# Hybrid decoder layer: two prompt softmax steps inside the query projection, cached-key scores in pairs of sequences

## The chip, the cores and the metric

The kernel runs on one core of a Trainium2 chip. Its engines are PE (TensorE: matrix products and transposes into PSUM), DVE (VectorE), ACT (ScalarE), POOL (GpSimd) and SP (SyncE, which here only issues DMA transfers). Each engine takes its instructions strictly in the order in which they are queued; semaphores hold an instruction until what it needs is there, and everything behind it on that engine waits too. The metric is the device time of one execution in microseconds (us); lower is better.

## The reference

One decoder layer for a prompt (512 rows of 1024) and a sample group (8 sequences of 4 new rows) with the same weights: a mixer, cross-attention into 256 memory tokens, and a gated ConvFFN. The change lies in the cross-attention:

```
def mem_attend(h, mk, mv, w_mq, w_mo):
    q = (h @ w_mq).reshape(B, T, MEM_HEADS, MEM_HEAD_DIM)        # 4 heads x 256
    s = jnp.einsum('bqhd,bkhd->bhqk', q, mk) * (MEM_HEAD_DIM ** -0.5)
    p = jax.nn.softmax(s, axis=-1)
    o = jnp.einsum('bhqk,bkhd->bqhd', p, mv).reshape(B, T, D_MODEL)
    return o @ w_mo
...
x = x + rms_norm(mem_attend(rms_norm(x, g_mem_pre), mk, mv, w_mq, w_mo), g_mem_post)
```

For the prompt, mk and mv come from the prompt's own memory (computed earlier in the kernel). For the samples they are caches, `cache_mem_k` and `cache_mem_v`: 8 sequences x 256 tokens x 4 heads x 256, 1 MB per sequence each for keys and values, read from HBM in this stage.

## The kernel before

The program is written as a straight sequence of calls. A scheduler orders them per engine when the kernel is built: it follows the written order, but lets an instruction pass others when its inputs and a free buffer are there earlier. `tc.issue_after` and `burst` tie an instruction behind another on the same engine. Tiles come from pools with a fixed number of buffers: `mm` (5 PSUM tiles for products), `W` (4 weight slots, reused here for cached keys and values), `st` (6 staging tiles of 512 KB), `S`, `N` and `Z`. A tile can be written again only when all readers of its former contents are done.

The stage of the change, in the written order:

- Query projection. `gemmB` (L485; L472 for the first four blocks) forms the queries transposed, in 8 column blocks m of w_mq, with 3 products for each pair of operands (high and low parts). `ev_q(m)` takes a block out of PSUM: `qh` on ScalarE (L1429), the low part `ql` on Vector (L1430), and the 32 sample rows `qs` on ScalarE (L1432). For the second four blocks `gemmB` is a generator that yields four times per block, so i = 0..15 counts its quarters.
- `mq_spread(h)`, called when head h's two blocks are out, copies that head's sample queries into block-diagonal tiles `qx`: heads 0 and 1 into the first (L1418), heads 2 and 3 into the second, `both` (L1415). It has 16 copies for heads 2 and 3 each, in four groups g of four.
- The prompt pipe, `prompt = pipe(8, ch_soft, ..., ch_turn, ch_out)`. A step i is half of the prompt rows of head i // 2. `next(prompt)` does `ch_out` of step i - 3, `ch_turn` of step i - 2 and `ch_soft` of step i. `ch_soft`: 12 score products `sca` (L1450), the maximum `cnm` on Vector (L1453), exp on ScalarE (L1456), the reciprocal (L1457) and the scaling of the rows `cp` on Vector (L1459). `ch_turn`: four PE transposes `cpt` of the rows (L1468), split into high and low parts `pT` (ScalarE L146, Vector L147). `ch_out`, every second step: 12 products `cpo` with the values (L1480), split into `oT`.
- The samples. `mk_load(b)` requests the keys of sequence b (L1498), 512 KB at a time: b = 0..2 into staging tiles (`wst`), b = 3..6 into weight slots and b = 7 into an `S` tile (`kvt`). `mk_turn(b)` turns them in place on Vector (L1502). `mk_scores` makes 32 products `ssc` for a sequence (L1519; each stands as two records in the trace) and ScalarE copies them to `sc` (L1521). `mk_sum` sums over groups into `pS` (L1535), `mem_softmax` takes the softmax (`spc`, L1550 to L1556, on Vector and ScalarE), turns it on PE (`spt`, L1565) and copies it into `caz` (L1568), `mv_load(b)` requests the values (L1576), and `mv_out` multiplies (`pso`, L1586).
- Then the output projection with w_mo (`gemmA`, L411 to L413).

Before, the keys' scores are made in two lots, sequences 0 to 2 and 3 to 7, after three prompt steps that stand behind the whole projection. Of head 3's sixteen query copies, eight are on GpSimd, four on Vector (g = 2) and four on ScalarE (g = 3).

Of the kernel before, what the change touches and what calls it, by code (L numbers as in the profile page):

```python
# [18 lines left out]
NB = 8  # L19
# [58 lines left out]
def kernel(ctx: ExitStack, tc: tile.TileContext, I, O):  # L78
    nc = tc.nc
# [22 lines left out]
    def S(shape, dt, name):  # L102
        return sp.tile(list(shape), dt, name=name, tag="S")
# [4 lines left out]
    def T2(shape, name, dt=F32):  # L108
        return t2p.tile(list(shape), dt, name=name, tag="T2")
# [7 lines left out]
    def mmp(name="mm"):  # L117
        return psm.tile([P, 512], F32, name=name, tag="mm")
# [4 lines left out]
    def view(t, off, dims, p=None):  # L123
        a = t.ap[0]
        return bass.AP(t.tensor, t.offset + off, [(a[0], a[1] if p is None else p)] + [tuple(d) for d in dims])

    def v2(t, b):
        return t.rearrange("p (a b) -> p a b", b=b)
# [7 lines left out]
    VCP = nc.vector.tensor_copy  # L136
# [72 lines left out]
    def stage():  # L209
        return stg.tile([P, 1024], F32, name="wst", tag="st")  # L210
# [133 lines left out]
    @contextmanager  # L344
    def burst(ins):

        if ins is None:
            yield
        else:
            with tc.issue_after(ins), tc.high_priority():  # L350
                yield
# [23 lines left out]
    def pipe(n, *stages):  # L375

        for t in range(n + len(stages) - 1):
            for s in reversed(range(len(stages))):
                if 0 <= t - s < n:
                    stages[s](t - s)  # L380
            yield
# [80 lines left out]
    def gemmB(xt, evacs, half_first=False):  # L462

        if half_first:
            slots = [W.get() for _ in evacs]
            for i, (c0, c1) in enumerate(HALF):
                for s, ev in zip(slots, evacs):
                    ps = mmp()[:, :c1 - c0]

                    for k0, l, x in ((0, 0, xt.hi), (0, 1, xt.hi), (4, 0, xt.hi), (4, 1, xt.hi), (0, 0, xt.lo), (4, 0, xt.lo)):  # L470
                        for k in range(k0, k0 + 4):
                            done[0] = mm(ps, lhsT=s[:, l, k, :], rhs=x(k, c0, c1), start=(k == 0 and l == 0 and x == xt.hi),  # L472
                                         stop=(k == 7 and x == xt.lo))
                    if i == 1:
                        W.free()
                    ev(i, c0, c1, ps)
                    yield 2.6
            return
        for ev in evacs:
            s = W.get()  # L480
            ps = [mmp()[:, :c1 - c0] for c0, c1 in HALF]
            for k in range(8):
                for j, (l, x) in enumerate(((0, xt.hi), (0, xt.lo), (1, xt.hi))):
                    for i, (c0, c1) in enumerate(HALF):
                        mm(ps[i], lhsT=s[:, l, k, :], rhs=x(k, c0, c1), start=(k == 0 and j == 0), stop=(k == 7 and j == 2))  # L485
                if k % 2 == 1 and k < 7:
                    yield 1.36
            W.free()
            for i, (c0, c1) in enumerate(HALF):
                ev(i, c0, c1, ps[i])  # L490
            yield 1.36
# [38 lines left out]
    for b in range(2):  # L530
        kept.append(norm_turn(xms[b], P, "g_mem_src", memT, b * P))
        if b == 0:

            t = turned[0].ins
            fill = mmp("fill")
            for _ in range(NFILL):
                with burst(t):
                    t = mm(fill, lhsT=warm[:, 0:P], rhs=warm, start=True, stop=True).ins
# [132 lines left out]
    for c0, c1 in HALF:  # L671
# [5 lines left out]
        t = T2([64, n], "gt")  # L677
# [253 lines left out]
    for g in range(2):  # L931
        for h in range(0, H, 2):
            t = stage().rearrange("p (j b e) -> p j b e", j=2, b=4)
# [38 lines left out]
    t = None  # L972
    for h in range(H):
        with burst(t):
            t = mm(pg[NS * h:NS * h + NS, P:2 * P + 1], lhsT=sm_t[:, h, :], rhs=vNs[:, h, :], start=True, stop=True).ins
    for h in range(H):
        with burst(t):
            t = mm(pg[NS * h:NS * h + NS, 4:12], lhsT=qT[:, h, SEQ:], rhs=nT[:, h, :], start=True, stop=True).ins
    for b in range(NB):
        for h in range(H):  # L980
            with burst(t):
                t = mm(pi[NS * h:NS * h + NS, 0:P], lhsT=qzm[:, 256 * h + b * NS:256 * h + (b + 1) * NS],
                       rhs=csts[b // 4, h][:, b % 4, :], start=(b == 0), stop=(b == NB - 1)).ins
# [313 lines left out]
    prompt = pipe(4 * H, da_soft, lambda i: None, da_turn, da_av, da_end)  # L1297
# [110 lines left out]
    def mq_spread(h):  # L1408

        for g in range(4):  # L1410
            copy = VCP if h == 3 and g == 2 else nc.scalar.copy if h == 3 and g == 3 else nc.gpsimd.tensor_copy
            for j in range(4):
                o, q = slice(NS * g, NS * g + NS), v2(qs[NS * j:NS * j + NS, 2 * h:2 * h + 2].rearrange("p c r -> p (c r)"), TS)
                if h // 2:
                    copy(out=both[o, :, j, :, h % 2, g, :], in_=q.rearrange("p (c n) t -> p c n t", c=2))  # L1415
                else:
                    for c in range(2):
                        copy(out=qx[0][c][o, j, :, h % 2, g, :], in_=q[:, NB * c:NB * c + NB])  # L1418

    def ev_q(m):  # L1420
        if m % 2 == 0:
            qh.append(npool.tile([P, 2, 516], F32R, name="qh", tag="N"))
        if m % 4 == 0:
            ql.append(S([P, 4, SEQ], F32R, "ql"))

        def ev(i, c0, c1, ps):
            n = min(c1, SEQ) - c0
            q = qh[m // 2][:, m % 2, c0:c0 + n]
            nc.scalar.mul(out=q, in_=ps[:, :n], mul=1.0 / 16.0)  # L1429
            STT(out=ql[m // 4][:, m % 4, c0:c0 + n], in0=ps[:, :n], scalar=1.0 / 16.0, in1=f32(q), op0=MUL, op1=SUB)  # L1430
            if i == 1:
                nc.scalar.mul(out=qs[:, m, :], in_=ps[:, n:n + NS], mul=1.0 / 16.0)  # L1432
                if m % 2 == 1:
                    mq_spread(m // 2)
        return ev
# [51 lines left out]
    def two(i):  # L1487

        if i < 3:
            return [stage(), stage()]  # L1490
        t = wp.tile([P, 2, DM], F32, name="kvt", tag="W") if i < 7 else S([P, 2, DM], F32, "kvt")
        return [t[:, 0], t[:, 1]]

    def mk_load(b):

        kst[b] = two(b)
        for c in range(2):
            dma(out=kst[b][c], in_=I["cache_mem_k"][0, b, c * P:(c + 1) * P].rearrange("t h d -> t (h d)"))  # L1498

    def mk_turn(b):  # L1500
        for t in kst[b]:
            nc.vector.transpose(out=t, in_=t)  # L1502

    def mk_scores(bs):

        t = None
        for b in bs:
            ps = mmp("ssc")[:, :256]
            for e in range(2):
                o = ps[:, e * P:e * P + P].rearrange("p (h c t) -> p h c t", h=2, c=2)  # L1510
                for c in range(2) if b < 3 else (None,):
                    for j in range(8):
                        g = NS * (j % 4)
                        if c is None:
                            w, k = o[g:g + NS], view(kst[b][0], 512 * e + NS * j, [(256, 2), (DM, 2), (1, NS)])
                        else:
                            w, k = o[g:g + NS, :, c], view(kst[b][c], 512 * e + NS * j, [(256, 2), (1, NS)])
                        with burst(t):
                            t = mm(w, lhsT=qx[e][j // 4][:, j % 4, b].rearrange("p e g t -> p (e g t)"), rhs=k,  # L1519
                                   start=(j < 4), stop=(j >= 4)).ins  # L1520
            nc.scalar.copy(out=sc[:, b], in_=ps)  # L1521
        return t
# [49 lines left out]
    def mv_load(b):  # L1572

        vts[b] = two(b)
        for c in range(2):
            dma(out=vts[b][c], in_=I["cache_mem_v"][0, b, c * P:(c + 1) * P].rearrange("t h d -> t (h d)"))  # L1576
# [12 lines left out]
    prompt = pipe(8, ch_soft, lambda i: None, ch_turn, ch_out)  # L1589
# [4 lines left out]
    for i, _ in enumerate(gemmB(hqT, [ev_q(m) for m in range(4, 8)])):  # L1594
        if i % 4 == 1 and i < 12:
            mk_turn(i // 4)
        if i % 4 == 3:
            mk_load(3 + i // 4)
    mk_load(7)

    next(prompt)
    next(prompt)
    next(prompt)
    sc = S([P, NB, 256], F32, "sc")
    mk_scores(range(3))
    for b in range(3):
        mv_load(b)
    for b in range(3, 8):
        mk_turn(b)
    t = mk_scores(range(3, 8))  # L1610
    for b in range(3, 8):
        mv_load(b)
    next(prompt)
    mk_sum(t)
    with tc.high_priority():
        az = mem_softmax()
# [203 lines left out]
    for gi, js in enumerate(groups):  # L1820
# [49 lines left out]
        if not last:  # L1870
            behind = []
            for n0 in (0, 512):
# [4 lines left out]
                for i in range(nk):  # L1877
# [3 lines left out]
                    for b in range(4):  # L1881
                        t = one(b, ps[b], i, s)
# [63 lines left out]
        t = chunk(TORD[1], 0)  # L1946

        for n0 in (0, 512):
            with burst(t.ins):
                t = chunk(TORD[0], n0)  # L1950
# [79 lines left out]
```

## Time and profile before

| | before |
|---|---|
| median of 3 runs | 948.5 us (947.84 to 948.78) |
| profiled execution | 948.29 us |
| its span, first to last instruction | 946.5 us |
| PE busy in the span | 915.8 us (97%) |
| Vector busy | 610.4 us (64%) |
| ScalarE busy | 378.1 us (40%) |
| GpSimd busy | 222.5 us (24%) |
| mean granted clock of PE | 0.991 |

The profile is one execution, recorded per engine. A row of the chain reads: start, duration, engine, output tile, line, number of records. A row of the timeline has start, busy time, engine, line, operation, out<-in, the shapes and the count, and in brackets the idle time of the engine before it with what ended it. "issue" means that the engine waited for nothing that the profile shows. PE has its weight loads (PEld) recorded apart from the products. A row of stretches gives for each engine the busy time and the number of records, then the granted PE clock (1 is full speed), the share of time that the DMA engines were busy, and GB/s.

### The profile page before, as it was taken

To read this page: it belongs to the slowest core of one execution; us is meant where nothing else is said; L and a number is where in the kernel's file an instruction comes from. 1 tells how busy PE (TensorE), PEld (TensorE's weight loads), DVE (VectorE), ACT (ScalarE), POOL (GpSimd) and SP (SyncE) were. 2 spreads that over 40 slices of the span, in tenths; PEclk is the share of its full clock that TensorE was granted. 3 is DMA by queue.
4 is the path that set the end of the run, shared out by engine and by line. 5 is a ranking of instruction groups with operands and counts; after the bars stand their busy time and mean duration, and the time that the engine had idled before them with its cause. 6 is when DMAs were issued, how large, how long until landed. Compare 5 with 4: busy or idle time off the path is not lost.

```text
span 946.5 us, 17459 instructions
## 1 busy us (share of the span) xinstructions
PE 915.8 (97%) x6778; PEld 800.7 (85%) x6778; DVE 610.4 (64%) x1134; ACT 378.1 (40%) x724; POOL 222.5 (24%) x474
## 2 busy tenths in 40 slices
PE   8999999999999999995999999999999999999994
PEld 5899787889866778995777899989988998999974
DVE  5845145565886448675554778737758775676767
ACT  5745134344676357513444533332212222222232
POOL 6610000025432217371000444001100110110114
PEclk9999999999999999998999999999999999999998
DMA  9950023343870539865854733062053303413023
GB/s 285 308 186 2 2 88 137 89 134 130 280 253 7 177 99 339 261 227 198 311 178 121 208 130 90 18 171 82 5 155 110 96 24 105 141 48 89 24 93 116
DMA packets 120835, 130.59 MB, mean 138 GB/s; under 512 B 8600, under 2 KB 86265, under 8 KB 120753
## 3 DMA queue, kind: packets, MB, share of 16 engines
q1 hardware_dynamic: 114568, 125.96, 42.5%
q10 hardware_dynamic: 6184, 3.53, 1.2%
q8 instruction: 53, 0.87, 0.4%
q14 instruction: 30, 0.24, 0.1%
HBM read 112.54 MB, written 16.93 MB: 137 GB/s over the span
## 4 chain that ended last, share of the span: by engine, by line
PE 86%; DVE 6%; DMA 3%; ACT 1%; issue 1%; POOL 0%; SPq 0%; DVEq 0%; ACTq 0%; POOLq 0%
PE mm L485 32%; PE mm L412 7%; PE mm L413 7%; PE mm L411 7%; PE mm L472 6%; PE mm L1836 3%; PE mm L1840 3%; PE mm L1839 3%; PE sda L1256 2%; PE mm L390 1%; PE cpo L1480 1%; PE sca L1450 1%; PE ssc L1519 1%; PE oda L1284 1%; DVE wslot L147 1%
## 5 line engine op out<-in xcount | busy, mean ns | idle before, releaser
L485 PE MATMUL mm<-fT,wslot 128*128 128x256 f32 x1872 | 235.9, 288 | 0.0
L485 PEld LDWEIGHTS mm<-fT,wslot 128*128 128x128 f32 x1872 | 234.4, 188 | 1.8 <-issue 0.8
L146 ACT CAST wslot<-wst 128x1024 fp32r<-128x1024 f32 x125 | 130.3, 1049 | 252.6 <-issue 77.4
L147 DVE TENSOR_TENSOR wslot<-wst,wslot 128x1024 fp32r<-128x1024 f32 x125 | 154.3, 1240 | 76.8 <-ACT wslot L146 76.6
L1836 PE MATMUL mm<-wslot,act 128*128 128x512 f32 (+1 forms) x180 | 69.3, 387 | 0.0
L1839 PE MATMUL mm<-wslot,act 128*128 128x512 f32 (+1 forms) x172 | 67.0, 391 | 0.0
L1840 PE MATMUL mm<-wslot,act 128*128 128x512 f32 (+1 forms) x172 | 66.8, 392 | 0.0
L1738 POOL COPY cvo<-u 128x2 f32<-128x2 f32 x43 | 10.5, 243 | 217.0 <-DVE u L1736 217.0
L411 PE MATMUL mm<-wslot,hT 128*128 128x512 f32 x128 | 51.3, 402 | 0.0
L413 PE MATMUL mm<-wslot,hT 128*128 128x512 f32 x128 | 51.0, 399 | 0.0
L485 PE MATMUL mm<-hT,wslot 128*128 128x256 f32 (+1 forms) x384 | 50.9, 289 | 0.0
L412 PE MATMUL mm<-wslot,hT 128*128 128x512 f32 x128 | 50.8, 397 | 0.0
L485 PEld LDWEIGHTS mm<-hT,wslot 128*128 128x128 f32 x384 | 49.2, 188 | 0.5 <-issue 0.2
L1733 DVE TENSOR_TENSOR u<-mm,rsb 128x256 f32<-128x256 f32 x43 | 18.2, 424 | 48.8 <-PE mm L485 48.7
L1836 PEld LDWEIGHTS mm<-wslot,act 128*128 128x128 f32 x180 | 34.3, 191 | 8.0 <-issue 0.4
L1840 PEld LDWEIGHTS mm<-wslot,act 128*128 128x128 f32 x172 | 32.3, 188 | 6.9 <-issue 0.4
L1839 PEld LDWEIGHTS mm<-wslot,act 128*128 128x128 f32 x172 | 32.3, 188 | 6.9
L1750 ACT ACTIVATE c<-c 128x560 f32<-128x560 f32 x21 | 14.1, 672 | 56.8 <-DVE c L1744 56.7
L1744 DVE SCALAR_TENSOR_TENSOR c<-u,cvT,c 128x560 f32<-128x560 f32 x43 | 34.3, 798 | 0.9
L1743 DVE SCALAR_TENSOR_TENSOR c<-u,cvT,c 128x560 f32<-128x560 f32 x43 | 34.1, 794 | 0.2
L1851 DVE TENSOR_TENSOR yp<-mm,yp 128x512 f32<-128x512 f32 (+1 forms) x41 | 27.1, 673 | 5.1 <-PE mm L1840 5.1
L413 PEld LDWEIGHTS mm<-wslot,hT 128*128 128x128 f32 x128 | 24.1, 188 | 5.0
(494 smaller groups left out, 1863.7 us busy)
## 6 DMA issues: line engine op xcount, KB each, us to landing
wst<-in_w_up_dram SPq DMA_DIRECT2D x42, 512.0 KB
wst<-in_w_in_dram SPq DMA_DIRECT2D x28, 512.0 KB
wst<-in_w_down_dram SPq DMA_DIRECT2D x20, 512.0 KB
kvt<-in_cache_mem_k_dram SPq DMA_DIRECT2D x10, 512.0 KB
kvt<-in_cache_mem_v_dram SPq DMA_DIRECT2D x10, 512.0 KB
wst<-in_w_mk_dram SPq DMA_DIRECT2D x8, 512.0 KB
xb<-in_x_prompt_dram SPq DMA_DIRECT2D x8, 512.0 KB
wst<-in_cache_dk_dram SPq DMA_DIRECT2D x16, 256.0 KB
```

What stands on the lines that cost most here:

```text
L146: nc.scalar.copy(out=hi, in_=src)
L147: (eng or nc.vector).tensor_tensor(out=lo, in0=src, in1=f32(hi), op=SUB)
L411: mm(ps[b], lhsT=xt.hi(k, c0, c0 + n), rhs=s[:, 0, kk, :], start=(k == 0), stop=False)
L412: mm(ps[b], lhsT=xt.hi(k, c0, c0 + n), rhs=s[:, 1, kk, :], start=False, stop=False)
L413: return mm(ps[b], lhsT=xt.lo(k, c0, c0 + n), rhs=s[:, 0, kk, :], start=False, stop=(k == nk - 1))
L472: done[0] = mm(ps, lhsT=s[:, l, k, :], rhs=x(k, c0, c1), start=(k == 0 and l == 0 and x == xt.hi), stop=(k == 7 and x == xt.lo))
L485: mm(ps[i], lhsT=s[:, l, k, :], rhs=x(k, c0, c1), start=(k == 0 and j == 0), stop=(k == 7 and j == 2))
L1743: STT(out=c, in0=u[:, 1:EXT - 1], scalar=w[1], in1=c, op0=MUL, op1=ADD)
L1744: STT(out=c, in0=u[:, 0:EXT - 2], scalar=w[0], in1=c, op0=MUL, op1=ADD)
L1836: mm(ps, lhsT=t[:, 0, c0:c0 + P], rhs=s[:, 0, i % 2, cs], start=st, stop=False)
L1839: mm(ps, lhsT=t[:, 0, c0:c0 + P], rhs=s[:, 1, i % 2, cs], start=False, stop=False)
L1840: return mm(ps, lhsT=t[:, 1, c0:c0 + P], rhs=s[:, 0, i % 2, cs], start=False, stop=en)
```

## The change

It does four things. The first two prompt steps move into the second half of the projection: after quarter 9 (middle of block 6) and after quarter 13 (middle of block 7). The scores of the cached keys are made in pairs of sequences, (0, 1), (2, 3), (4, 5), (6, 7), with one prompt step after each of the first three pairs, and the values of a pair are requested right behind its scores. The keys of sequences 3 to 7 are turned between the pairs in the written order. And the four copies of head 3's queries with g = 2 go from Vector to ScalarE.

```diff
     def mq_spread(h):
         for g in range(4):
-            copy = VCP if h == 3 and g == 2 else nc.scalar.copy if h == 3 and g == 3 else nc.gpsimd.tensor_copy
+            copy = nc.scalar.copy if h == 3 and g > 1 else nc.gpsimd.tensor_copy
...
     for i, _ in enumerate(gemmB(hqT, [ev_q(m) for m in range(4, 8)])):
...
         if i % 4 == 3:
             mk_load(3 + i // 4)
+        if i in (9, 13):
+            next(prompt)
+
     mk_load(7)
-
-    next(prompt)
-    next(prompt)
     next(prompt)
     sc = S([P, NB, 256], F32, "sc")
-    mk_scores(range(3))
-    for b in range(3):
+    for b in range(0, NB, 2):
+        t = mk_scores((b, b + 1))
         mv_load(b)
-    for b in range(3, 8):
-        mk_turn(b)
-    t = mk_scores(range(3, 8))
-    for b in range(3, 8):
-        mv_load(b)
-    next(prompt)
+        mv_load(b + 1)
+        if b < 6:
+            if b:
+                mk_turn(b + 2)
+            mk_turn(b + 3)
+            next(prompt)
     mk_sum(t)
```

What the scheduler makes of it is seen in the queues. On PE, the cached keys' scores stood in two runs of 96 and 80 products with three transposes between them (before):

```order
L1519 MATMUL ssc<-wst,qx 32x2x32 x96
L1468 MATMUL cpt<-cpk,cp 128x128 x3
L1519 MATMUL ssc<-kvt,qx 32x128 x80
L1468 MATMUL cpt<-cpk,cp 128x128 x4
```

After the change, PE has at the second pair (sequence 2 from staging tiles, sequence 3 from a slot), with prompt products on both sides:

```order
L1450 MATMUL sca<-mkT,ql 128x256
L1519 MATMUL ssc<-wst,qx 32x2x32 x32
L1519 MATMUL ssc<-kvt,qx 32x128 x16
L1480 MATMUL cpo<-pT,mvN 128x512 x12
L1468 MATMUL cpt<-cpk,cp 128x128 x4
```

No run of scores has more than 64 products now, and each is followed by value products, transposes or prompt scores.

On Vector, at the end of the query projection (before; the first row is the evacuation of block 6's queries, the third that of block 7's):

```order
L1430 SCALAR_TENSOR_TENSOR ql<-mm,qh 128x256 x2
L1502 STREAM_TRANSPOSE kvt<-kvt 128x1024 x3
L1430 SCALAR_TENSOR_TENSOR ql<-mm,qh 128x256 x2
L1453 TENSOR_REDUCE cnm<-sca 128x2
L1502 STREAM_TRANSPOSE kvt<-kvt 128x1024
L1415 COPY qx<-qs 32x2x8x4 x4
L1453 TENSOR_REDUCE cnm<-sca 128x2
L1502 STREAM_TRANSPOSE kvt<-kvt 128x1024
L1457 RECIPROCAL csu<-csu 128x2
```

The same place after the change:

```order
L1430 SCALAR_TENSOR_TENSOR ql<-mm,qh 128x256 x2
L1502 STREAM_TRANSPOSE kvt<-kvt 128x1024 x2
L1453 TENSOR_REDUCE cnm<-sca 128x2
L1502 STREAM_TRANSPOSE kvt<-kvt 128x1024
L1457 RECIPROCAL csu<-csu 128x2
L1502 STREAM_TRANSPOSE kvt<-kvt 128x1024
L1459 TENSOR_SCALAR cp<-cp,csu 128x256 x2
L1430 SCALAR_TENSOR_TENSOR ql<-mm,qh 128x256 x2
L147 TENSOR_TENSOR pT<-cpt,pT 128x256
L1453 TENSOR_REDUCE cnm<-sca 128x2
```

Block 7's evacuation now stands behind the second prompt step's maximum, reciprocal and scaling and behind both transposes of sequence 7's keys; the four query copies are gone from Vector. The transposes of sequence 6's keys follow next, and on SP the request of these keys stands behind six loads of the convolution's state.

On PE, around the turned sample softmax `spt` (before):

```order
L1480 MATMUL cpo<-pT,mvN 128x512 x8
L1565 MATMUL spt<-cpk,spc 32x32 x32
L1480 MATMUL cpo<-pT,mvN 128x512 x4
L1468 MATMUL cpt<-cpk,cp 128x128 x4
L1450 MATMUL sca<-mkT,qh 128x256 x2
```

The same place after the change:

```order
L1480 MATMUL cpo<-pT,mvN 128x512 x12
L1468 MATMUL cpt<-cpk,cp 128x128 x4
L1565 MATMUL spt<-cpk,spc 32x32 x32
L1586 MATMUL pso<-wst,caz 32x256 x24
L1468 MATMUL cpt<-cpk,cp 128x128 x4
```

The value products of the samples (`pso`) follow `spt` directly; before, four prompt products, four transposes and twelve prompt scores lay between. Vector's last softmax step (L1556) now stands behind the output difference of the first of the twelve `cpo` groups, and two scaling pairs where there was one.

## Prediction

> **What bounds the kernel now.** I read the page first: the span and the busy shares.
>
> ```profile
> span 946.5 us, 17459 instructions
> PE 915.8 (97%) x6778; PEld 800.7 (85%) x6778; DVE 610.4 (64%) x1134; ACT 378.1 (40%) x724; POOL 222.5 (24%) x474
> ```
>
> PE is the bound: it is idle for 30.7 us of the span and nothing else is near it. So the change can win only PE's idle or slow time. The waits of PE, longest first, say where most of the idle time is: one wait of the prompt's transposes (cpt) for the scaled softmax rows (cp).
>
> ```profile
> PE cpt L1468 <- DVE cp L1459: 7.5, 1, 7.5
> ```
>
> Third, the chain that ended last, from the end of the query projection on (start, duration, what).
>
> ```profile
> 424.12 3.54 DMA kvt<-in_cache_mem_k_dram
> ...
> 427.79 1.25 DVE kvt L1502
> 429.03 0.64 DVE ql L1430 x2
> 429.67 0.60 DVE cnm L1453
> ...
> 432.20 1.84 DVE qx L1415
> ...
> 437.68 0.45 PE cpt L1468
> 438.13 2.56 PE sca L1450 x12
> 440.69 2.53 PE ssc L1519 x160
> 443.22 1.68 issue
> 444.90 0.65 PE ssc L1519 x32
> 445.55 0.48 PE cpt L1468 x3
> 446.03 2.75 PE ssc L1519 x93
> 448.78 3.06 issue
> 451.83 3.36 PE ssc L1519 x67
> 455.19 0.59 PE cpt L1468 x4
> 455.78 1.43 PE sca L1450 x12
> 457.21 2.39 PE pS L1535 x32
> 459.60 2.99 PE cpo L1480 x12
> ...
> 468.18 0.69 PE spt L1565 x50
> ...
> 471.85 2.73 PE pso L1586 x48
> ```
>
> The reader is to see three losses. PE stands still from 437.68 - 7.5 = 430.1 while Vector turns keys, copies queries (1.84 for one copy) and only then scales the softmax rows. Then the twelve score products take 2.56 us, though the same twelve take 1.43 at 455.78. And the cached keys' scores (ssc) stop twice, 1.68 and 3.06 us, waiting for nothing that the profile shows; the 67 records after the second stop take 3.36 us where 93 took 2.75. The clock column (next to last but two) of the stretches of 5 us explains the slow ones:
>
> ```profile
> 435.00:440.00 5.00, 2.32 (x11) 2.35 (x12) 3.32 (x8) 0.83 (x4) 0.00 (x0) 0.50 0.17 39
> 450.00:455.00 5.00, 3.17 (x67) 2.90 (x67) 0.00 (x0) 0.74 (x2) 0.00 (x0) 0.66 0.88 324
> ```
>
> The granted clock is halved after the first standstill and for part of the time after the last.
>
> **What the change removes.** Two prompt steps stand inside the projection, so their scaled rows are ready when PE first wants to turn them, and scores come in four short runs. Against full-speed rows:
>
> - the standstill: 7.5;
> - its slow clock: 2.56 - 1.43 for the scores, and 0.3 for the lone transpose (0.45, where four take 0.59): 1.4;
> - the two stops: 1.68 + 3.06 = 4.7;
> - slow records after the second: 3.36 - 67 x 2.75/93 = 1.4.
>
> Together 15.0 us. The two steps' own 2 x 1.43 us only change place on PE: projection and both steps still end at 430.1.
>
> **What it adds.** (1) The queries of the last head. The scores need qx complete, and the last head's part hangs on the projection's last evacuation. In the new Vector order this evacuation (ql) stands behind the transposes of sequence 7's keys and a softmax scaling. These rows price the pieces:
>
> ```profile
> 429.71 0.20 ACT L1432 ACTIVATE qs<-mm 128x32 f32<-128x32 f32 x1 [1.86 <-DVE ql L1430]
> 429.99 1.04 ACT L1415 COPY qx<-qs 32x64 f32<-32x64 f32 x4
> 429.96 2.17 POOL L1415 COPY qx<-qs 32x64 f32<-32x64 f32 x8 [5.71 <-ACT qs L1432]
> 432.20 1.80 POOL L1558 MEMSET caz<- 128x2048 f32 x1
> 437.20 1.12 DVE L1459 TENSOR_SCALAR cp<-cp,csu 128x256 f32<-128x256 f32 x4
> ```
>
> Sequence 7's keys landed at 424.12 + 3.54 = 427.66. Their buffer comes free in the middle of the last query block, which now has one prompt step more ahead of it: 427.66 + 1.43 = 429.1. Vector: two transposes, 2 x 1.25, to 431.6; half of the 1.12 scaling, to 432.2; ql, 0.64, to 432.8. ScalarE: qs 0.20, which waits for ql as its row shows, and now eight copies, 2 x 1.04, to 435.1; GpSimd's eight take 2.17, beside them. With some 0.05 us for each of six hand-overs: 435.4. PE comes there at 430.1 + 0.59 + 1.43, does the first sixteen products, which need only heads 0 and 1 (0.5, as 32 of 160 records in 2.53), and stands at 432.6. Wait: 2.8, rounded up to **3.0** because the second half of these keys may land later than the first. Bounds: 1.0, if Vector is free when the projection ends (then only ql, qs and the copies remain, 430.1 to 433.3, and hand-overs); 4.0, if the keys land a microsecond later. That two copies leave Vector is worth nothing beyond this: the row of 1.84 ran beside the 1.80 memset of GpSimd, which the new order puts later.
>
> (2) The clock after that wait. The nearest row is the 3.06 stop, with 1.4 us lost after it. I take **1.3**; bounds 0 and 1.4. [...]
>
> (3) The stops. Between them PE ran 32 + 3 + 93 = 128 product records, each with a weight load: 256. The page's instruction queue and two windows of the DMA view (441 to 443, 448 to 452):
>
> ```profile
> q8 instruction: 53, 0.87, 0.4%
> q8 instruction: 1, 0.02, 4.2%
> q8 instruction: 1, 0.02, 1.4%
> ```
>
> 2 x 6778 PE records over 53 packets are 256 each, and one packet lies in each of the two windows, just before PE goes on. So I read the stops as waits for code: 256 records took 3.7 us from block to block the first time (128 records before 443.22 at 2.53/160 each, plus 1.68) and 0.65 + 0.48 + 2.75 + 3.06 = 6.9 the second time, with the DMA engines full of values. In the new order the densest 128 products after the first loads of values are about 111 score records, four transposes and twelve prompt scores: 111 x 2.75/93 + 0.59 + 1.43 = 5.3 us. Cost: 0 to 1.6; the loads of values run there, so nearer the second row: **1.2**.
>
> (4) The sample softmax. Rows, Vector's first, then ScalarE's:
>
> ```profile
> 459.71 0.42 DVE L1552 TENSOR_REDUCE spc<-pS 128x4 f32<-128x256 f32 x1 [1.60 <-PE pS L1535]
> ...
> 463.25 0.69 DVE L147 TENSOR_TENSOR oT<-cpo,oT 128x512 fp32r<-128x512 f32 x1 [0.31 <-ACT oT L146]
> ...
> 467.05 0.40 DVE L1556 TENSOR_TENSOR spc<-spc 128x256 f32<-128x256 f32 x1
> ...
> 472.49 0.41 DVE L147 TENSOR_TENSOR pT<-cpt,pT 128x256 fp32r<-128x256 f32 x1
> ...
> 471.84 0.37 ACT L146 CAST pT<-cpt 128x256 fp32r<-128x256 f32 x1 [0.92 <-DVE pT L147]
> ...
> 468.97 0.43 ACT L1568 COPY caz<-spt 128x128 f32<-128x128 f32 x2 [0.80 <-PE spt L1565]
> ```
>
> On Vector it took 459.71 to 467.45, 7.7 us, under 468.18 - 459.60 = 8.6 us of prompt work on PE. The new order puts three more things ahead of its last step (L1556): one output difference (0.69), one of P (0.41), one scaling pair (0.56). 7.7 + 1.7 = 9.4. PE's cover has 17 value products for 20 (-0.75) and four transposes more (+0.5): 8.35. PE waits **1.1** for spt (0.8 to 1.4, as Vector's own idle in that stretch shrinks or not). Then pso follows spt at once; before, products and a prompt step lay between. The copies of spt (0.43) now stand on ScalarE behind a cast that waits for Vector's next output and P differences: 0.69 + 0.41 + 0.37 + 0.43 and hand-overs, 2.0, less spt's own 0.8: **1.2** more (0.5, if only the copy shows, to 1.5). Two idle pieces so near each other may halve the clock: **0.4** (0 to 1.4).
>
> (5) At nothing: the values' loads now wait each for its own pair's scores, the last at about 453, and are needed past 468; a load of this size took 3.54. GpSimd's memset of 1.80 comes later but long before 468. The output projection's weights wait for pso to free staging buffers:
>
> ```profile
> 479.59 4.63 DVE L147 TENSOR_TENSOR wslot<-wst,wslot 128x1024 fp32r<-128x1024 f32 x4 [0.38 <-ACT wslot L146]
> ```
>
> The first is ready at 479.6 + 1.2, 6.2 us after pso's first run ends (471.85 + 2.73). In the new order 0.59 + 80 x 2.73/48 + 2.99 = 8.1 us of PE work lie there: covered with 1.9 to spare. If that cover went, the projection would start late by the difference.
>
> Sum: 15.0 - (3.0 + 1.3 + 1.2 + 1.1 + 1.2 + 0.4) = 15.0 - 8.2 = 6.8 us. PE stays the bound afterwards, so it reaches the end. The profiled execution took 948.29 (span 946.5 and 1.8 around it): 941.5. It is 0.2 below the median of the three runs, so **941.7** against 948.5. All low ends together give 938, all high ends 946.
>
> **Rivals.** Faster: Vector is free earlier and code is hidden. Then (1) falls to 1.0, and (2) and (3) vanish: 941.7 - 4.5 = 937.2. For it: Vector was idle in front of transposes before, waiting for keys; against: it now has two softmax steps to do in the same stretch.
>
> The stops remain. If they belong to the score products and not to code, shorter runs do not cure them: 1.68 + 3.06 + 1.4 come back in place of (3): 941.7 + 6.1 - 1.2 = 946.6. For it: nothing names the releaser. Against: the 256 records. [...]
>
> Slower: sequence 6's keys. They are requested behind six small convolution loads, and Vector's queue holds their transposes ahead of P's second difference, which a PSUM tile of the next scores waits for (needed at 435.4 + 0.5 + 1.0 + 1.3 + 0.6, about 439). Two transposes and the difference, 2.9, stand between: each microsecond of landing past 436 costs one. Slower than 950.4 needs 8.7 lost, a landing at about 445: against it, 3.54 from request to landing, and even twice that from 430.1 is 437.2. It would give 951.
>
> **How the numbers follow.** Forecast 0.62 (939 to 946); faster rival 0.15; stops remain 0.16; keys late 0.07. The range goes from the fast rival to past the third: 937.0 to 947.5. What a measurement tells from no change is about 0.2%, 1.9 us: faster is below 946.6. The forecast, the fast rival and a third of the stops' case give 0.82; the rest of that case and a little of the last, 0.12; slower 0.06.
>
> **What would show it.** PE's 7.5 wait for cp gone and the two score groups among L485; a PE wait of about 3 us in ssc for qx, released by ScalarE or GpSimd; "issue" in ssc under 2 us in all; waits of about 1 us each ahead of spt and pso; the output projection (L411) starting some 5 us earlier. Wrong would be: a stop of 2 us or more in the new ssc runs without a releaser, a wait in the projection itself for a PSUM tile that Vector has not freed, or gains there that come back as waits in the output projection.

## The result and the profile after

| | before | after |
|---|---|---|
| median | 948.78 us (947.84 to 951.18, 5 executions) | 943.26 us (941.59 to 945.0, 5 executions) |
| ratio to before, 95% interval | | 0.994 (0.992 to 0.9959) |
| profiled execution, its span | 948.29, 946.5 us | 941.59, 939.8 us |
| stage: first product of the second half of the query projection (L485) to the first `rsb` (L1704) | 403.18 to 540.1: 136.9 us | 403.90 to 534.0: 130.1 us |
| the rest, from there to the end of the span | 406.4 us | 405.8 us |

The forecast was 941.7 us, 937.0 to 947.5, faster with 0.82: the measured median is 1.6 us above it. The stage row gives the comparison free of what varies ahead of it (in the profiles shown here, the second half of the projection starts anywhere from 402.95 to 405.02 us in kernels that share the code up to there).

The page after: PE is still the bound, with 1.3 us less busy time and 5.4 us less idle time.

```profile
span 939.8 us, 17453 instructions
PE 914.5 (97%) x6778; PEld 799.9 (85%) x6778; DVE 608.5 (65%) x1130; ACT 378.2 (40%) x728; POOL 221.6 (24%) x474
```

The waits of PE that the stage has now (line, releaser, us in total, times, longest). The wait for `cp` and the "issue" of 4.7 us are gone; these three stand in their place.

```profile
PE ssc L1519 <- POOL qx L1415: 3.7, 1, 3.7
PE pso L1586 <- ACT caz L1568: 1.0, 1, 1.0
PE spt L1565 <- DVE spc L1556: 0.8, 1, 0.8
```

The new largest wait, in the timeline of Vector, ScalarE, GpSimd and PE (start, duration, engine, line, count, and in brackets the engine's idle time before it and what ended it):

```profile
433.07 1.25 DVE L1502 STREAM_TRANSPOSE kvt<-kvt 128x1024 f32<-128x1024 f32 x1 [1.43 <-DMA kvt<-in_cache_mem_k_dram]
434.24 0.57 DVE L1459 TENSOR_SCALAR cp<-cp,csu 128x256 f32<-128x256 f32 x2
434.73 0.74 DVE L1430 SCALAR_TENSOR_TENSOR ql<-mm,qh 128x256 fp32r<-128x256 f32 x2
435.50 0.20 ACT L1432 ACTIVATE qs<-mm 128x32 f32<-128x32 f32 x1 [3.26 <-DVE ql L1430]
435.76 2.16 POOL L1415 COPY qx<-qs 32x64 f32<-32x64 f32 x8 [10.94 <-ACT qs L1432]
432.86 0.65 PE L1519 MATMUL ssc<-wst,qx 128*32 128x64 f32 x32
437.19 3.56 PE L1519 MATMUL ssc<-wst,qx 128*32 128x64 f32 x96 [3.67 <-POOL qx L1415]
```

It is the chain that the prediction set out: transposes of sequence 7's keys, scaling, `ql`, `qs`, copies. Only the keys' second half landed 1.43 us after Vector was ready for it. The 96 records behind the wait take 3.56 us, where 160 took 2.53 before. In part they wait for one copy after another, in part the clock is halved (stretches of 5 us; the granted clock stands before the DMA share and GB/s), from 437.88 to 441.29. The last two rows are PE's alone, for the stretch ahead of the slow one and for the slow one:

```profile
435.00:440.00 5.00, 2.81 (x82) 2.44 (x86) 4.41 (x9) 3.78 (x15) 1.82 (x8) 0.79 0.53 144
440.00:445.00 5.00, 5.00 (x138) 4.50 (x128) 1.83 (x5) 2.15 (x8) 0.00 (x0) 0.87 0.89 291
434.46:437.88 3.42, 0.69 (x6) 1.00 0.67 198
437.88:441.29 3.41, 3.41 (x95) 0.50 0.46 117
```

PE does not wait for all copies: it goes on at 437.19, while GpSimd copies until 435.76 + 2.16 = 437.92.

The two smaller waits, and the output projection's first product, which started at 486.16 before:

```profile
469.10 0.76 PE L1565 MATMUL spt<-cpk,spc 128*32 128x32 f32 x64 [0.84 <-DVE spc L1556]
470.82 2.80 PE L1586 MATMUL pso<-wst,caz 128*32 128x256 f32 x48 [0.96 <-ACT caz L1568]
481.49 0.63 PE L411 MATMUL mm<-wslot,oT 128*128 128x512 f32 x2
```

### The profile page after: what moved, and what is told of

Its sections match the earlier page's. It is cut to its first block, busy times and chain, and to the rows that moved or that the text cites. A ratio compares the mean times of both kernels' runs of the same rounds, so it can differ in the third digit from the quotient of the medians.

```text
span 939.8 us, 17453 instructions
## 1 busy us (share of the span) xinstructions
PE 914.5 (97%) x6778; PEld 799.9 (85%) x6778; DVE 608.5 (65%) x1130; ACT 378.2 (40%) x728; POOL 221.6 (24%) x474
## 5 line engine op out<-in xcount | busy, mean ns | idle before, releaser
L485 PE MATMUL mm<-fT,wslot 128*128 128x256 f32 x1872 | 236.0, 288 | 0.0
L485 PEld LDWEIGHTS mm<-fT,wslot 128*128 128x128 f32 x1872 | 234.4, 188 | 1.8 <-issue 0.8
L1738 POOL COPY cvo<-u 128x2 f32<-128x2 f32 x43 | 10.4, 242 | 217.2 <-DVE u L1736 217.2
L485 PE MATMUL mm<-hT,wslot 128*128 128x256 f32 (+1 forms) x384 | 50.9, 289 | 0.0
L485 PEld LDWEIGHTS mm<-hT,wslot 128*128 128x128 f32 x384 | 49.2, 188 | 0.5 <-issue 0.2
```

## Experiments

Each was timed beside the kernel before on the same chip (whose median there was 948.5 to 950.8 us); the ratio is to those executions. "Stage" is the profiled execution's, as above; the waits are PE's, in us.

| kernel | median us | ratio (95%) | stage | cpt for cp | ssc for qx | issue in ssc | spt + pso |
|---|---|---|---|---|---|---|---|
| before | 948.78 | 1 | 136.9 | 7.5 | 0 | 4.7 | 0 |
| after | 943.26 | 0.994 (0.992 to 0.9959) | 130.1 | 0 | 3.7 | 0 | 1.8 |
| after, measured again | 942.84 | 0.9933 (0.9913 to 0.9954) | 131.3 | 0 | 3.3 | 0 | 1.8 |
| steps only | 944.33 | 0.9935 (0.991 to 0.996) | 131.0 | 0 | 3.5 | 2.1 | 0 |
| pairs only | 944.11 | 0.9943 (0.9924 to 0.9962) | 132.5 | 5.9 | 0 | 0 | 1.8 |
| copies back on Vector | 944.12 | 0.9928 (0.9902 to 0.9955) | 131.7 | 0 | 3.3 | 0 | 1.8 |
| last query first | 940.76 | 0.9882 (0.9851 to 0.9912) | 130.3 | 0 | 1.3 | 0 | 1.8 |
| sample softmax first | 939.69 | 0.9916 (0.9902 to 0.993) | 127.7 | 0 | 3.0 | 0 | 0.4 |
| sample rows first | 939.3 | 0.9895 (0.9872 to 0.9918) | 127.1 | 0 | 0.4 | 0 | 1.8 |
| sample rows and softmax first | 937.49 | 0.989 (0.9874 to 0.9905) | 125.5 | 0 | 0.2 | 0 | 0.4 |

### The steps alone

The kernel before, with only this:

```diff
+        if i in (9, 13):
+            next(prompt)
...
     mk_load(7)
-    next(prompt)
-    next(prompt)
     next(prompt)
```

> The kernel before with only the two prompt steps moved into the query projection (after quarters 9 and 13); scores still in lots of three and five sequences, copies on Vector. Theory (the two edits act apart: the steps remove the standstill, the short runs remove the code stops): the 7.5 us wait of cpt for cp and its slow clock (1.4) go; a wait of about 3.5 us for qx and about 1.5 us of slow clock come; 176 score products now follow each other without anything between, so 'issue' in ssc stays at 4 to 7 us in all. Net gain 3 to 4: 944.5 to 946. Rival (the stops were an after-effect of the standstill, and go with it): no 'issue' over 0.5 us in ssc, and the gain is 9 to 10: 939 to 940.

Measured 944.33 us. The standstill went and the wait for `qx` came, 3.45 us, as expected by the theory; of the stops one remained, 2.15 us, less than the 4 to 7 expected. PE's rows:

```profile
437.41 5.23 PE L1519 MATMUL ssc<-wst,qx 128*32 128x64 f32 x159 [3.45 <-DVE qx L1415]
447.45 2.16 PE L1519 MATMUL ssc<-kvt,qx 128*32 128x128 f32 x67 [2.15 <-issue]
```

The stop stands 67 records before the end of the scores, exactly where the second one stood before. The first had no chance to show: the wait of 3.45 us lies in the 128 records that end where it stood, and most of the rest ran at half clock (5.23 us for 159, where 160 took 2.53 before), so they took 7.7 us, where the 128 up to the second stop before took 6.9 with the stop at their end: time enough for the next code, by the prediction's reading of the stops. So the steps remove part of the stops by themselves (4.7 - 2.15 = 2.6 us, and 3.36 - 2.16 = 1.2 us of the slow records behind the second), and that is why the two halves of the change do not add.

### The pairs alone

The kernel before, with the new loop over pairs of sequences; the first three steps stay behind the projection and the four copies stay on Vector.

```diff
     next(prompt)
     next(prompt)
     next(prompt)
...
-    mk_scores(range(3))
-    for b in range(3):
+    for b in range(0, NB, 2):
+        t = mk_scores((b, b + 1))
         mv_load(b)
-    for b in range(3, 8):
-        mk_turn(b)
-    t = mk_scores(range(3, 8))
-    for b in range(3, 8):
-        mv_load(b)
-    next(prompt)
+        mv_load(b + 1)
...
```

> The kernel before with only the scores in pairs of sequences between prompt steps; the first two prompt steps still behind the projection, copies on Vector. Theory: the wait of cpt for cp stays at 7 to 8 us with its half clock, the wait for qx stays hidden behind it (under 0.5 us), 'issue' in ssc is under 0.5 us in all, and the waits of spt and pso (together about 1.8 us) come: a gain of 6.1 - 1.8 = 4.3, so 944 to 945. Rival (the stops belong to the score products themselves): 'issue' of 3 to 5 us stays in ssc, and the time is 948 to 950.

Measured 944.11 us, as the theory has it: no stop, the two new waits of 0.84 and 0.96 us, and the standstill (5.9, somewhat short of the 7 to 8 expected).

```profile
437.47 0.45 PE L1468 MATMUL cpt<-cpk,cp 128*128 128x128 f32 x1 [5.92 <-DVE cp L1459]
440.41 2.22 PE L1519 MATMUL ssc<-wst,qx 128*32 128x64 f32 x128
471.04 0.76 PE L1565 MATMUL spt<-cpk,spc 128*32 128x32 f32 x64 [0.84 <-DVE spc L1556]
```

By the stage, the steps alone are worth 6.0 us, the pairs alone 4.4, and both 6.8 (5.6 when measured again), not 10.4. With the steps in place the pairs add 0.9 us or nothing: they take away the stop of 2.15 and give back 1.8 at `spt` and `pso`.

### The copies

```diff
-            copy = nc.scalar.copy if h == 3 and g > 1 else nc.gpsimd.tensor_copy
+            copy = VCP if h == 3 and g == 2 else nc.scalar.copy if h == 3 and g == 3 else nc.gpsimd.tensor_copy
```

> The changed kernel with the four query copies of g = 2 back on Vector. Theory: the wait for qx ends with GpSimd's eight copies (2.16 us) whatever ScalarE does, so the wait stays at 3.5 to 4 us and the time at 942 to 944, ratio to the changed kernel 0.998 to 1.002; Vector's four copies (about 1 us) only delay sequence 6's transposes, which cost nothing. Rival (taking the copies off Vector pays by itself): 1 to 2 us slower than the changed kernel, 944.5 to 945.5, with a wait of PE for a tile that Vector frees.

Measured 944.12 us. The wait is 3.3 us, and one of Vector's copies ends it now, not GpSimd's as the theory had it; it is no longer for that. So the move of the copies off Vector is worth nothing that this can tell, as the theory and the prediction had it.

### Whether ql sets qx

```diff
     def mk_turn(b):
-        for t in kst[b]:
-            nc.vector.transpose(out=t, in_=t)
+        with tc.issue_after(qlast[0].ins) if b == 7 else nullcontext():   # the last ql
+            for t in kst[b]:
+                nc.vector.transpose(out=t, in_=t)
```

> The changed kernel with the transposes of sequence 7's keys tied behind the last query evacuation (ql) on Vector. Theory (the wait for qx hangs on ql, which stands behind two transposes of 1.25 us and a wait of 1.4 us for their keys): ql ends about 2.7 to 3.9 us earlier, the wait for qx falls from 3.7 to 0 to 1.2 us, no half-clock window follows (1.5 us), and the time is 4 to 5 us below the changed kernel: 938 to 940. Rival 1 (GpSimd's or ScalarE's copies are the bound): the wait stays over 2.5 us, time within 1 us of the changed kernel. Rival 2 (the delay moves on to the turned keys): the wait for qx falls, but PE waits 2 us or more for kvt of sequences 6 and 7 at the last pair, time 941 to 943.

Measured 940.76 us, a little above the 938 to 940 expected and 3.4 below "copies back" on the same chip. The wait fell to 1.27 us and the records behind it ran at full clock; nothing came back at the last pair. But the profiled execution's stage is only as long as after's (130.3), because it lost 1.7 us at another place, and 1.2 us of waiting for an earlier `ql`:

```profile
436.13 2.34 PE L1520 MATMUL ssc<-wst,qx 128*32 128x64 f32 x96 [1.27 <-POOL qx L1415]
467.16 0.76 PE L1566 MATMUL spt<-cpk,spc 128*32 128x32 f32 x64 [0.84 <-DVE spc L1557]
468.88 4.48 PE L1587 MATMUL pso<-wst,caz 128*32 128x256 f32 x48 [0.96 <-ACT caz L1569]
```

The same 48 records of `pso` took 2.80 us in the kernel after. The waits ahead of them are the same to 0.01 us. The stretches that end with the clock's changes tell the difference (us, PE busy, granted clock, DMA share, GB/s), for this kernel and then for the one after:

```profile
465.66:469.07 3.41, 1.61 (x73) 1.00 1.03 420
469.07:472.48 3.41, 3.41 (x36) 0.50 0.59 187
```

```profile
465.18:468.60 3.42, 3.08 (x16) 1.00 1.03 411
468.60:472.01 3.41, 1.95 (x88) 1.00 0.50 195
```

In this stage the clock changed only at borders a whole number of 3.41 us apart (it was halved from 433.86 to 440.69 and from 450.93 to 454.34 before, from 437.88 to 441.29 after), and these lie elsewhere against the kernel's work from profile to profile. Here both waits fell into one such window, PE was busy for 1.61 us of it, and the next window ran at half clock (0.50). After, a border lay elsewhere, the same waits left 1.95 us busy, and the clock stayed at 1.

### What the stops are

First the values' loads were written behind all scores (in the kernel before):

```diff
-    for b in range(3):
-        mv_load(b)
...
-    for b in range(3, 8):
+    for b in range(8):
         mv_load(b)
```

> The kernel before with all eight sequences' values requested behind the last score product instead of behind each lot. Theory (the two stops are waits for the next block of code, stretched by the values' loads that keep the DMA engines full): with the engines free the 128 records between the two stops take longer (3.9 us) than a quiet fetch (3.7 us from block to block), so the second stop falls from 3.1 us to under 0.6 and the 1.4 us of slow records behind it go; the first stop, which had little traffic, stays between 1 and 2 us. Rival (the stops belong to the score products or to their result tiles): 1.7 and 3.1 us as before, at the same places. In both, the values come some 7 us later, and PE may wait for them in pso, so the time itself (945 to 950) does not decide.

Measured 948.37 us. The edit did not do what it was for. SyncE's queue only waits for free buffers, so the loads still ran beside the scores (DMA share 1.00 below), and the stops were 0.79 and 3.61 us. With a ratio of 0.9997 (0.9985 to 1.0008) the time tells nothing apart either.

```profile
450.00:455.00 5.00, 2.03 (x73) 1.76 (x65) 0.58 (x2) 1.02 (x3) 0.00 (x0) 1.00 1.00 387
455.64 3.47 PE L1519 MATMUL ssc<-kvt,qx 128*32 128x128 f32 x67 [3.61 <-issue]
```

The second try issued them from ScalarE, behind its copy of the last scores:

```diff
+            done[0] = nc.scalar.copy(out=sc[:, b], in_=ps).ins
...
+    with tc.issue_after(done[0]):
+        for b in range(8):
+            mv_load(b)        # nc.scalar.dma_start
```

> The kernel before with all values' loads issued from ScalarE's queue, tied behind its copy of the last sequence's scores, so that none can start before the score products are done. Theory (the stops are waits for the next block of code, stretched by these loads): at both borders the DMA engines are now nearly idle; the first stop, after 160 records, falls from 1.7 to 1 us or less and the second, 67 records before the end, from 3.1 to 1 us or less. Rival (fetching a block takes that long on quiet DMA engines too): stops of 1.5 us or more at the same places. ScalarE issues 16 transfers ahead of its next work and the values come some 8 us later, so the time will be worse (950 to 960) in both and decides nothing.

Now the DMA engines are quiet at both borders (share 0.01 in the stretch), the first stop is 0.91 us and the second is gone: the 160 records run through at the pace of the undisturbed ones before (4.74 us; 160 x 2.75/93 = 4.73). The time, 959.42 us, is worse for the reason given: PE waits 10.6 us for a cast that stands behind ScalarE's sixteen loads.

```profile
446.29 0.65 PE L1519 MATMUL ssc<-wst,qx 128*32 128x64 f32 x32 [0.91 <-issue]
447.36 4.74 PE L1519 MATMUL ssc<-kvt,qx 128*32 128x128 f32 x160
445.00:450.00 5.00, 4.09 (x158) 3.68 (x150) 0.85 (x2) 2.14 (x6) 0.00 (x0) 1.00 0.01 3
```

Third, the place. 64 products ahead of everything shift PE's stream by 128 records against the blocks (their results are not used):

```diff
+    for _ in range(64):
+        mm(wps[:, :8], lhsT=warm[:, 0:P], rhs=warm[:, :8], start=True, stop=True)
```

> The kernel before with 64 tiny extra products (8 columns, result never used) in the warm-up at the very start: 128 more records in PE's stream, half a block of 256. Theory (stops stand at the borders of code blocks): both borders move 64 product records earlier, so the first stop comes after about 96 score records instead of 160, and the second one 131 records before the end of the scores instead of 67; packets of the instruction queue move with them. Rival (the stops belong to the scores' tiles or to their place in the program): both stops stay after 160 records and 67 before the end. Time within 2 us of the kernel before in both.

```profile
449.08 3.05 PE L1521 MATMUL ssc<-wst,qx 128*32 128x64 f32 x192
452.06 0.55 PE L1470 MATMUL cpt<-cpk,cp 128*128 128x128 f32 x3
452.53 1.07 PE L1521 MATMUL ssc<-kvt,qx 128*32 128x128 f32 x29
455.50 5.36 PE L1521 MATMUL ssc<-kvt,qx 128*32 128x128 f32 x128 [1.90 <-issue]
461.69 0.41 PE L1521 MATMUL ssc<-kvt,qx 128*32 128x128 f32 x3 [0.83 <-issue]
```

The stops moved: none after 160 records or 67 before the end. They stand after 192 + 3 + 29 = 224 records and 128 later, which are the expected borders (96, 224, 352). At 96, where the expectation wanted the first stop, there is none: the standstill of 8.1 us lies in the block before that border, and the packet of the next block landed at 437.69, some 13 us before PE came to it. Both points show code and not the scores' tiles. The time, 954.55 us, was expected within 2 us of before and was not: this kernel's projection half starts 7.3 us later (410.50), while its stage (137.6) is before's. What of those 7.3 us the 64 products cost themselves, and what comes from borders that moved ahead of it, no run separates.

The instruction queue shows the link itself. It has one packet for each 128 products with their weight loads (53 packets before, for 6778 products). Eight such stops stand in these profiles: two each in the kernel before, with later values and with shifted code, one each in the steps alone and with the values behind. In all eight PE goes on 1.4 to 1.6 us after the packet of the next block has landed, whether the stop lasted 0.79 or 3.61 us. The second stop before is an example: its packet ran from 449.40 to 450.31, and PE went on at 451.83. What differs is how late the packet starts: 0.6 to 1.1 us behind the border before it with the DMA engines idle or half busy, 1.9 to 5.1 us with them at 0.88 of their time or more.

The same count finds the borders where nothing stopped. These are the 128 products up to the second stop before, and the densest 128 of the kernel after and of the pairs alone (us, PE busy, granted clock, DMA share, GB/s):

```profile
444.90:451.83 6.93, 3.88 (x128) 0.94 0.97 359
450.17:455.49 5.32, 5.32 (x138) 1.00 0.96 357
452.10:457.42 5.32, 5.32 (x137) 1.00 1.04 409
```

The DMA engines were as full in all three (a packet is counted whole where it starts, so a share can pass 1). After, the next packet still came early, from 449.68 to 450.72: the DMA engines had been idle from 448 to 449 (share 0.01), between the loads of two pairs' values. In the pairs alone it landed at 455.79, so with the 1.4 to 1.6 us that follow the code was there at most 0.2 us before PE came to the border.

### The two waits at the sample softmax

The kernel after, with three orders fixed: Vector's L1556 ahead of the `oT` differences, ScalarE's `caz` copies ahead of the next casts, and of the two copies the one that VORD needs first.

```diff
+            with tc.issue_after(smx[0]) if i == 5 else nullcontext():    # L1556
                 put(oT, h // 2, j, j + 1, 0, SEQ, po.unsqueeze(1))
...
+        with tc.issue_after(smx[1]) if i == 6 else nullcontext():        # the caz copies
             for c in range(2):
                 split(...)                                               # cpt to pT
...
-        for c in range(2):
+        for c in (1, 0):
             nc.scalar.copy(out=view(az, c * 1024, ...
```

> The changed kernel with three orders fixed by hand: Vector's last sample softmax step (L1556) ahead of the output differences that stood before it, ScalarE's copies of spt into caz ahead of the casts of the next transposes, and the copy that the first value product needs made first. Theory (the two waits come from what is queued ahead on Vector and ScalarE): the wait of spt falls from 0.8 to under 0.3, that of pso from 1.0 to 0.6 or less, and no half-clock window follows them: 1 us less than the changed kernel's best executions, 1.5 to 2 in the mean, ratio to the kernel before 0.991 to 0.993. Rival (the chain of the softmax itself is that long): both waits stay near 0.8 and 1.0, ratio 0.994.

Measured 939.69 us. `spt` no longer waits and `pso` waits 0.41 us:

```profile
467.94 0.77 PE L1567 MATMUL spt<-cpk,spc 128*32 128x32 f32 x64
469.12 0.64 PE L1589 MATMUL pso<-wst,caz 128*32 128x256 f32 x8 [0.41 <-ACT caz L1570]
438.25 2.32 PE L1521 MATMUL ssc<-wst,qx 128*32 128x64 f32 x96 [3.05 <-POOL qx L1415]
```

So these waits were what was queued ahead of the softmax. The last row shows the windows' luck once more: here even a wait of 3.05 us was followed by full clock (2.32 us for the 96 records, 3.56 in the kernel after), and it had fallen into two windows, with PE busy for 1.70 and 2.08 us. That is a part of this stage's 127.7, and no run shows it to be a gain of this edit.

### The sample rows first, and the change measured again

ScalarE's `qs` waited for Vector's `ql` though it needs nothing of it; it reads the same PSUM tile and was written behind it. The kernel after, with this alone:

```diff
+            if i == 1:
+                nc.scalar.mul(out=qs[:, m, :], in_=ps[:, n:n + NS], mul=1.0 / 16.0)
             STT(out=ql[m // 4][:, m % 4, c0:c0 + n], ...)
-            if i == 1:
-                nc.scalar.mul(out=qs[:, m, :], in_=ps[:, n:n + NS], mul=1.0 / 16.0)
```

> The changed kernel with one edit: ScalarE takes a block's sample rows qs out right behind qh, ahead of Vector's ql. Theory (the wait for qx is 3.7 us because qs waits for ql): the wait falls under 1 us, no half-clock window follows it, and the waits of spt and pso (0.8 and 1.0, with a half-clock window of 1.7 us in some executions) stay: 3.5 to 5 us below the changed kernel, ratio to the kernel before 0.989 to 0.991. Rival (the softmax kernel and this edit overlap, since the time that is won at qx is lost again at spt): under 2 us below it, ratio 0.992 to 0.994, with a longer wait at spt.

> The changed kernel itself, for a second look beside the others: 941 to 945, ratio to the kernel before 0.992 to 0.996, waits of 3.3 to 3.9 (qx), 0.8 (spt) and 1.0 us (pso). Theory (a half-clock window follows only where a window of 3.4 us was busy for less than about half): whether the value products pso take 2.8 or 4.5 us changes from execution to execution with where the waits fall in the windows. Rival (the difference belongs to the kernels): 2.8 us again.

Measured 939.3 us against 942.84 for the kernel after beside it: 3.5 us, the lower end of the expectation. `ql` ends as late as ever, but the copies no longer ask for it:

```profile
432.29 0.21 ACT L1431 ACTIVATE qs<-mm 128x32 f32<-128x32 f32 x1
432.57 2.19 POOL L1415 COPY qx<-qs 32x64 f32<-32x64 f32 x8 [12.09 <-ACT qs L1431]
434.84 0.75 DVE L1432 SCALAR_TENSOR_TENSOR ql<-mm,qh 128x256 fp32r<-128x256 f32 x2
434.19 2.30 PE L1520 MATMUL ssc<-wst,qx 128*32 128x64 f32 x96 [0.40 <-POOL qx L1415]
```

In the kernel after measured again, `pso` again took 2.80 us; its window was busy for 1.77 of 3.41. So within one kernel the change from 2.8 to 4.5 was not caught; the comparison of kernels with the same two waits speaks for it. The mean granted clocks of single executions fit it: 0.992 to 0.997 in the five of "sample softmax first", where one window at half clock makes 3.41/2/938 = 0.002. They do not show where the windows lay.

### Both

> The orders of the softmax kernel, and the sample rows qs of each block taken out by ScalarE right behind qh, ahead of ql instead of behind it. Theory (the wait for qx hangs on qs, which waited for ql on Vector behind keys that were still landing): the last copies of qx end about 2.5 to 3.3 us earlier against the end of the projection, PE's wait for qx falls from 3.7 to 0.3 to 1.2 us, no half-clock window follows (1.5 us), and the time is 4 to 6 us below the changed kernel: ratio to the kernel before 0.986 to 0.989. Rival (something else on GpSimd or Vector sets qx): the wait stays above 2.5 us, ratio 0.991 to 0.994.

The last two edits together: 937.49 us, the lowest median, and the shortest stage, 125.5 us. The ratio, 0.989, is not told apart from that of "last query first" (0.9882, 0.9851 to 0.9912), which was timed on another chip. It is the upper end of what was expected (0.986 to 0.989). No wait of PE in this stage is longer now than 0.6 us.

## Why the prediction held, step by step

The forecast's sum for the stage was 15.0 - 8.2 = 6.8; the profiled stage became 136.9 - 130.1 = 6.8 shorter. That the figures agree is partly luck, since terms erred on both sides:

- What is removed, 15.0: shown. The standstill and both stops with their slow records are gone from the chain. The runs also show that it was not one sum: the steps alone remove the first stop and 0.9 us of the second too.
- (1) Last head's queries, 3.0: it was 3.67, and 3.32 when measured again. The mechanism held, and "last query first" and "sample rows first" show its links; the term is short by the keys' landing, which came 1.43 us after Vector was ready and not before. The bound of 4.0 had been set for that. But the term has a second part: the prediction let PE wait until all copies were done, while PE went on early and then took the copies one by one. At full clock the 96 records behind the wait took 2.30 to 2.34 us in three other kernels, against 96 x 2.53/160 = 1.52 without staggered copies: some 0.8 more. With it the term is 4.5, beyond its bound. (Four copies left Vector, not two as the prediction says; nothing hung on it.)
- (2) Clock after it, 1.3: the 96 records took 3.56 - 1.52 = 2.0 us too long and four transposes 0.93 for 0.60, together 2.4, of which the staggered copies are 0.8. That leaves 1.6. The row of before, 1.4 us lost after the stop of 3.06, was a fair guide; but the term is not a constant: 0 in "sample softmax first" with a wait of 3.05.
- (3) Code, 1.2: it was 0. This is the term that missed. The densest stretch took 5.32 us for the 5.3 expected, and the DMA engines were as full as the prediction feared. The step that failed is the 6.9 us as the price of a fetch under full load: after, the packet met a gap between two loads, and in the pairs alone, without such a gap, 5.32 us were just enough. So 0 is no safe price either. In "last query first" the packets landed 1.4 and 1.6 us ahead of two borders, and PE paused for 0.3 and 0.2 us there, too short for the table. What sets how long a packet waits behind the loads stays open.
- (4) `spt` 1.1 and `pso` 1.2: 0.84 and 0.96; clock 0.4: 0 here, 1.7 in two other kernels with the same two waits.
- (5) At nothing: held. The output projection starts 481.49 against 486.16. Sequence 6's keys, the slower rival, landed 0.55 us after Vector was ready, and PE did not wait for them.

Terms as measured: 4.5 + 1.6 + 0 + 0.8 + 1.0 = 7.9 for 8.2, which would make 7.1; the 0.3 to the stage's 6.8 is not placed. One sum of the prediction is wrong: its low ends together give 948.5 - (15.0 - 2.3) = 935.8 and its high ends 948.5 - (15.0 - 11.3) = 944.8, not 938 and 946. The median is further off, 943.26 for 941.7, since the profiled execution was the lowest of its five, while the forecast took its distance to the median from before. What differs between the profiles is the start of the stage (2 us), a wait of 0 to 1.2 us in L485 for `ql` behind keys that are still landing, and the clock's windows.

That wait in L485 is one of the prediction's signs of being wrong: 0 in the kernel after, 1.1 us when measured again. But the pairs alone (0.8) and the kernel with later values (1.0), whose steps stand behind the projection as before, have it too, so no run ties it to the change.

Of the rivals, "stops remain" is refuted by the pairs alone and by the quiet and shifted kernels. The faster rival's 937.2 was reached, by another way than it named: 937.49, once `qs` no longer waited for Vector and the softmax went first.

## What to carry to other kernels

When two parts of a change remove waits on the same engine, price them one on top of the other: a wait that goes uncovers the one that lay under it (here `qx`, hidden by the standstill) and may already take away another (here the first code stop). Ask of every wait that remains whether its releaser really needs what it waited for; `qs` stood behind `ql` only because it was written behind it, and that cost 3.5 us, more than half of what the whole change won. Look for runs of many short products beside full DMA engines: here 128 products that kept PE busy for 3.88 us at a DMA share of 0.97 ended in a stop of 3.06 us, which the runs trace to code that came late, and with longer products among them 128 took 5.32 us without such a stop. Break such a run up with long products, and expect the margin to be thin (0.2 us at most in the pairs alone).

## What the runs showed of the hardware

- The granted clock fell to 0.50 for windows of 3.41 us, here after windows in which PE had been busy for 0 and 1.26 us (the kernel before), 0.69 and 0.37 us (the kernel after, twice), 1.61 and 1.62 us (last query first, copies back) and 1.51 us (shifted code, after a stop of only 1.90 us). After 1.70 us (sample softmax first) and 1.77 and 1.95 us (the kernel after, twice) it stayed at 1. A window already at half clock was followed by another after 1.88 us (steps only), and by full clock after 2.51 and 3.01 us (the kernel before). The windows lie elsewhere against the kernel in each profile, so the same two waits cost 1.7 us in one (`pso` 4.48 us, last query first) and nothing in another (2.80 us, the kernel after).
- The eight stops of PE at a border between code blocks (256 records of PE, weight loads included: 53 packets for 6778 products) ended 1.4 to 1.6 us after the packet of the next block had landed. From the border before to the end of the stop it took 3.3 to 3.8 us with the DMA engines idle or half busy (shares 0.02 to 0.53: the first stops of the kernel before and of the two with later values) and 4.9 to 7.5 us with them full (0.88 to 1.02: shifted code, steps only, the second stops). Where the 256 records themselves lasted 5.32 us beside full DMA engines (0.96 in the kernel after, 1.04 in the pairs alone), PE did not stop.
